# Weight quadrants loaded three steps before their sums, and part of the sums moved from VectorE to GpSimd

## The chip, the cores and the metric

The kernel runs on one core of one Trainium2 chip. The core has TensorE (PE; its weight loads are PEld), VectorE (DVE), ScalarE (ACT), GpSimd (POOL) and SyncE (SP), which work side by side and wait for each other by semaphores; each takes its instructions in order. SP and GpSimd also issue DMAs, which sixteen DMA engines carry out. The metric is the device time of one execution in microseconds. The median of three runs of the kernel before is 2614.47 us (2612.9 to 2618.87).

## The reference

One layer of a decoder trunk over a prompt of 2048 tokens (from position 0, no state) and 64 sample tokens (8 sequences of 8, with state), all in float32:

```
z = rms_norm(x, pre_g);  proj = z @ w_in            # 2048 -> 5 x 1024: xr, gr, u, v, gs
xc = causal depthwise conv of width 4 over xr
r, i = sigmoid(xc @ w_r + b_r), sigmoid(xc @ w_i + b_i)          # 8 heads of 128
h = linear recurrence with a = exp(-8 r softplus(-lam)) over sqrt(1 - a^2) i xc
br = h * silu(gr)
v = rms_norm(gelu(v), sgu_g);  s = (masked w_s) v + b_s          # within chunks of 128 tokens
bs = gelu(u) * s * silu(gs)
y = x + rms_norm([br, bs] @ w_out, post_g)                       # 2048 -> 2048
```

The two large products (`w_in` and `w_out`) hold nearly all of the arithmetic. The outputs are y, the last conv rows and h, and the normalised v of the sample.

## The kernel before

The prompt is worked in four groups of 512 tokens; the first group also takes the 64 sample tokens. A float32 product is made of three passes of TensorE in a rounded format: each weight tile and each activation tile is split into a high half (rounded by ScalarE, line L184 for weights, as `wh_...`) and a low half (the rest, by VectorE, L192, as `wl_...`), and high x high, high x low and low x high are summed.

**Groups 1 to 3** multiply by a scheme with seven products of half-size blocks in place of eight. Of a unit (a 2 x 2 arrangement of weight blocks B11, B12, B21, B22, each 128x1024 here) it needs the four quadrants as they are and the four sums P1 = B11 + B12, P3 = B12 + B22, P2 = B22 + P1 and P4 = B21 + P2. There are 28 units: 16 of column blocks of `w_in` (kind `c`: xr with gr, u with gs), 4 of `w_v` and 8 of `w_or` (the same v and out weights, laid out by rows). The sums are the same for all three groups.

**The first group** multiplies plainly, and makes these sums on the side: `make_sums` loads a unit's four quadrants into SBUF (DMAs issued by GpSimd, line L235), adds them on VectorE (L241, L243, L245, L247), and stores each sum to DRAM (DMAs issued by GpSimd, L239), where later groups load it as they load any weight. The buffers are of the pool `dp` (tag `dbl`, 13 buffers), which the first group also uses for the gelu of v (3 for each of two halves, from the v stage until the spatial products are done), gate weights, squares, and later the statistics of group 1.

The first group's TensorE work goes by steps, one weight piece each (48 matmuls of 128x288, L363; 30 of 128x512 for v, L374). The jobs come in this order: xr and gr by head pairs with gates and recurrence between, v, then gs and u by head pairs with a spatial product for each head (`spatial_pe` L552, taken from PSUM by VectorE in `spatial_dve` L558), then the sixteen blocks of the output projection (`out`). A weight piece is loaded by SP (`wraw_...`, L176), rounded by ScalarE (L184) and has its low half made by VectorE (L192), three pieces ahead (LOOK = 3), in pools of three buffers. VectorE also evacuates products (`scaled`, L393).

Other work on GpSimd's queue in this group is: u times gs (L545), the gate product i times xc (L478), the stores of the branches to DRAM (`cat`, L500 and L578), their reloads ahead of the output projection (`cb`, L336), the stores of its blocks (L590) and the sums of their squares (L311), and from block 8 on the loads for the statistics of group 1 (`xs`, L613). From these statistics VectorE makes `xd` (L630), which TensorE spreads over the partitions (`nsx`, L635).

What sets the order: in the first group the program gives steps and side work in program order, and the framework's scheduler puts every engine's instructions in a fixed order, by priority (program order) and by its own estimate of when each is ready; so an instruction can be put well ahead of its place in the program where its engine and a buffer are free. `by_step` gives the place of each unit: with a clock of 6.3 us for a step (6.8 for v), unit n stands at the first step whose clock is at least 60 + 20.5 n. Groups 1 to 3 are in an order written out by hand (`manual_schedule`), and the change doesn't touch them.

Of the kernel before, what the change touches and what calls it, by code (L numbers as in the profile page):

```python
# [32 lines left out]
W = 1024  # L33
# [18 lines left out]
def hybrid_layer(ctx: ExitStack, tc: tile.TileContext, a):  # L52
    nc = tc.nc
# [18 lines left out]
    def dbl(name, dt=F32):  # L72
        return dp.tile([P, 2, DW], dt, tag="dbl", name=name)

    def flat(t, n):
        return t.rearrange("p a c -> p (a c)")[:, :n]
# [16 lines left out]
    side = nc.gpsimd  # L93
# [47 lines left out]
    state = {}  # L141
# [66 lines left out]
    def cm_src(w, j, i):  # L208
        return a[w][j][:, i * HALF:(i + 1) * HALF, :].rearrange("p a c -> p (a c)")

    def tm_src(w, j, i):
        return a[w][j, i].rearrange("p a c -> p (a c)")
# [6 lines left out]
    def quadrants(unit):  # L219
        kind, j, u = unit  # L220
        if kind == "c":
            return {"B11": cm_src("w_in", j, 0), "B21": cm_src("w_in", j, 1),
                    "B12": cm_src("w_in", j + 1, 0), "B22": cm_src("w_in", j + 1, 1)}
        return {"B11": tm_src(kind, 2 * j, u), "B21": tm_src(kind, 2 * j, 4 + u),
                "B12": tm_src(kind, 2 * j + 1, u), "B22": tm_src(kind, 2 * j + 1, 4 + u)}

    sums = {}

    def make_sums(unit):
        src = quadrants(unit)  # L230
        nm = "_".join(str(x) for x in unit)
        t = {}
        for b in ("B11", "B12", "B22", "B21"):
            t[b] = flat(dbl(f"p{b}{nm}"), W)
            side.dma_start(t[b], src[b])  # L235

        def put(k, x):
            sums[unit, k] = hp.tile([P, W], F32, name=f"{k}_{nm}")
            side.dma_start(sums[unit, k], x)  # L239

        nc.vector.tensor_add(t["B11"], t["B11"], t["B12"])  # L241
        put("P1", t["B11"])
        nc.vector.tensor_add(t["B12"], t["B12"], t["B22"])  # L243
        put("P3", t["B12"])
        nc.vector.tensor_add(t["B22"], t["B22"], t["B11"])  # L245
        put("P2", t["B22"])
        nc.vector.tensor_add(t["B21"], t["B21"], t["B22"])  # L247
        put("P4", t["B21"])

    def prod_src(unit, k):  # L250
# [814 lines left out]
    for s in steps:  # L1065
        for job, i in s:
            kind, j = job
            if is_v(job):
                src = lambda j=j, i=i: tm_src("w_v", j, i)
            else:  # L1070
                src = lambda w="w_out" if kind == "out" else "w_in", j=j, i=i: cm_src(w, j, i)
# [37 lines left out]
    for hp_ in range(0, NH, 2):  # L1109
        i = jobs.index(("gr", NH + hp_ + 1))  # L1110
# [13 lines left out]
    by_step = defaultdict(list)  # L1124
    clock, when = 0.0, []
# [1 line left out]
        when.append(clock)  # L1127
        clock += sum(6.8 if is_v(job) else 6.3 for job, _ in s)
    for n, u in enumerate(units):
        t = 60 + 20.5 * n  # L1130
        by_step[next(i for i, x in enumerate(when) if x >= t)].append((make_sums, u))
    for n in range(8):
        at(("out", 8 + n // 4), stat_load, 1, n)
        at(("out", 9 + n // 4), stat_sum, 1, n)
# [22 lines left out]
    for n, step in enumerate(steps):  # L1157
        for f, *args in by_step[n]:
            f(*args)
        job, i = step[0]  # L1160
# [31 lines left out]
    for g in range(1, NG):  # L1192
# [25 lines left out]
        if g == 1:  # L1218
            for j in range(KT):
                t = 4 + 3 * j // 2 if j < 10 else V + 11 + 2 * (j - 10)  # L1220
                at2(t, finish0_load, j)
                t = max(t + 3, 9)
# [179 lines left out]
```

## Time and profile before

| what | value |
|---|---|
| median of 3 runs | 2614.47 us |
| profiled execution, its own time | 2626.4 us |
| its span, first to last instruction | 2624.7 us |
| granted TensorE clock, mean over the span | 0.981 |
| mean DMA rate over the span | 224 GB/s |
| matmul instructions | 16710 |

The rows further down are of this one profiled execution. Times are microseconds from the start of the span, unless marked ns. The granted clock is a share of full speed: 1.00 is the level of 2.4 GHz, 0.50 that of 1.2 GHz, and a mean between them is a stretch that has both. A wait is the idle time of an engine just before an instruction, and behind the arrow stands what ended it. The first group lasts until about 824 us of the span, when the last block of its output projection is evacuated.

### The profile page before, as it was taken

Reading aid. Unit: us, or ns where it says so; the run is one execution under the profiler, and the core shown is the slowest. Engines: PE = TensorE matmul, PEld = TensorE weight load, DVE = VectorE, ACT = ScalarE, POOL = GpSimd, SP = SyncE. Lnnn points to the kernel's source line nnn. Section 1 sums busy time; section 2 is a strip of 40 time slices with the busy share of each in tenths; the row PEclk is TensorE's granted clock in tenths of the full one; section 3 lists DMA queues with packets and bytes.
Section 4 is the critical chain, followed back from the end, with each engine's and each line's share of the span. In section 5 each row is a group of like instructions: output and inputs, shape, how many; then the busy total and the mean of one; then the engine's idle time right before and its main releaser. Section 6 shows DMA issues by size and latency. Waiting matters only on the chain.

```text
span 2624.7 us, 41603 instructions
## 1 busy us (share of the span) xinstructions
PE 2515.9 (96%) x16710; PEld 2314.8 (88%) x16710; DVE 1761.6 (67%) x2284; ACT 1396.5 (53%) x1787; POOL 350.7 (13%) x504
## 2 busy tenths in 40 slices
PE   7999999899998999999999899999999999999996
PEld 6999789899998998799878898899878898899884
DVE  7786255545457777666789677666789677656865
ACT  5445332123233577645756477645756477645654
POOL 4331023322422200100100200000000200000000
PEclk9999999999998999999999999999999999999998
DMA  6995378865865855756775955555775955555576
GB/s 225 332 336 192 112 256 305 322 255 186 322 241 161 272 179 186 234 184 186 256 263 190 328 171 181 170 184 185 256 257 195 327 178 177 179 182 182 187 260 189
DMA packets 168673, 589.21 MB, mean 224 GB/s; under 512 B 19216, under 2 KB 19776, under 8 KB 168480
## 3 DMA queue, kind: packets, MB, share of 16 engines
q1 hardware_dynamic: 106544, 377.06, 43.1%
q0 software_dynamic: 60784, 207.40, 23.5%
q8 instruction: 130, 2.13, 0.3%
q10 hardware_dynamic: 1152, 2.10, 0.2%
q14 instruction: 63, 0.52, 0.1%
HBM read 494.92 MB, written 89.47 MB: 223 GB/s over the span
## 4 chain that ended last, share of the span: by engine, by line
PE 71%; DMA 10%; DVE 8%; ACT 5%; issue 4%; POOL 1%; SPq 0%; DVEq 0%; ACTq 0%; POOLq 0%
PE gm0out L363 7%; PE gm0v L374 4%; PE gm0gr L363 4%; PE gm0xr L363 2%; PE gm0gs L363 2%; DVE wl_c_B L192 1%; DMA wraw_c_P<-P_c 1%; PE gm0u L363 1%; DMA wraw_w_or_P<-P_w_or 1%; PE g L850 1%; DMA pB22w_v<-w_v 1%; DMA wraw_c_B<-w_in 1%; PE sp L552 1%; PE w3o1a L709 1%; PE w3vd L709 1%
## 5 line engine op out<-in xcount | busy, mean ns | idle before, releaser
L184 ACT ACTIVATE wh_c_P<-wraw_c_P 128x1024 fp32r<-128x1024 f32 x192 | 203.3, 1059 | 269.6 <-DMA wraw_c_P<-P_c 87.4
L192 DVE TENSOR_TENSOR wl_c_P<-wraw_c_P,wh_c_P 128x1024 fp32r<-128x1024 f32 x192 | 234.4, 1222 | 111.8 <-ACT wh_c_P L184 109.0
L192 DVE TENSOR_TENSOR wl_c_B<-wraw_c_B,wh_c_B 128x1024 fp32r<-128x1024 f32 x144 | 175.3, 1220 | 84.1 <-ACT wh_c_B L184 84.1
L184 ACT ACTIVATE wh_c_B<-wraw_c_B 128x1024 fp32r<-128x1024 f32 x144 | 152.1, 1057 | 140.6 <-DMA wraw_c_B<-w_in 46.9
L184 ACT ACTIVATE wh_w_or_P<-wraw_w_or_P 128x1024 fp32r<-128x1024 f32 x96 | 101.6, 1058 | 85.5 <-DMA wraw_w_or_P<-P_w_or 32.3
L192 DVE TENSOR_TENSOR wl_w_or_P<-wraw_w_or_P,wh_w_or_P 128x1024 fp32r<-128x1024 f32 x96 | 117.3, 1222 | 43.8 <-ACT wh_w_or_P L184 43.2
L184 ACT ACTIVATE wh_w_or_B<-wraw_w_or_B 128x1024 fp32r<-128x1024 f32 x72 | 76.3, 1059 | 85.3 <-DMA wraw_w_or_B<-w_or 17.5
L363 PE MATMUL gm0out<-c0l,wh_out 128*128 128x288 f32 x512 | 112.2, 300 | 1.4 <-DVE c0l L158 1.3
L192 DVE TENSOR_TENSOR wl_w_or_B<-wraw_w_or_B,wh_w_or_B 128x1024 fp32r<-128x1024 f32 x72 | 87.9, 1221 | 35.9 <-ACT wh_w_or_B L184 35.5
L363 PE MATMUL gm0out<-c0h,wl_out 128*128 128x288 f32 x512 | 110.8, 298 | 0.1
L363 PE MATMUL gm0out<-c0h,wh_out 128*128 128x288 f32 x512 | 110.7, 298 | 0.0
L363 PEld LDWEIGHTS gm0out<-c0l,wh_out 128*128 128x128 f32 x512 | 82.6, 190 | 2.9 <-DVE c0l L158 2.3
L363 PEld LDWEIGHTS gm0out<-c0h,wl_out 128*128 128x128 f32 x512 | 82.8, 190 | 0.8 <-issue 0.5
L363 PEld LDWEIGHTS gm0out<-c0h,wh_out 128*128 128x128 f32 x512 | 82.7, 190 | 0.1
L613 POOL DMA_DIRECT2D xs<-xt x24 | 12.8, 536 | 504.5 <-ACT wh_c_P L184 257.2
L192 DVE TENSOR_TENSOR wl_w_v_P<-wraw_w_v_P,wh_w_v_P 128x1024 fp32r<-128x1024 f32 x48 | 58.5, 1222 | 27.7 <-ACT wh_w_v_P L184 27.7
L184 ACT ACTIVATE wh_out<-wraw_out 128x1024 fp32r<-128x1024 f32 x32 | 33.7, 1056 | 81.3 <-PE gm0out L363 54.3
L184 ACT ACTIVATE wh_w_v_P<-wraw_w_v_P 128x1024 fp32r<-128x1024 f32 x48 | 49.9, 1054 | 47.2 <-DMA wraw_w_v_P<-P_w_v 31.9
L192 DVE TENSOR_TENSOR wl_out<-wraw_out,wh_out 128x1024 fp32r<-128x1024 f32 x32 | 41.0, 1283 | 41.3 <-ACT wh_out L184 41.2
L363 PE MATMUL gm0xr<-z0h,wh_xr 128*128 128x288 f32 x256 | 57.3, 306 | 7.9 <-ACT wh_xr L184 5.5
L374 PE MATMUL gm0v<-wh_v,z0l 128*128 128x512 f32 (+1 forms) x160 | 63.4, 396 | 0.0
L374 PE MATMUL gm0v<-wl_v,z0h 128*128 128x512 f32 (+1 forms) x160 | 63.1, 394 | 0.0
(1612 smaller groups left out, 8544.5 us busy)
## 6 DMA issues: line engine op xcount, KB each, us to landing
wraw_c_P<-P_c SPq DMA_DIRECT2D x192, 512.0 KB, 4.1
wraw_c_B<-w_in SPq DMA_DIRECT2D x144, 512.0 KB, 4.2
wraw_w_or_P<-P_w_or SPq DMA_DIRECT2D x96, 512.0 KB, 4.3
wraw_w_or_B<-w_or SPq DMA_DIRECT2D x72, 512.0 KB, 4.2
wraw_w_v_P<-P_w_v SPq DMA_DIRECT2D x48, 512.0 KB, 3.6
wraw_w_v_B<-w_v SPq DMA_DIRECT2D x36, 512.0 KB, 3.4
wraw_out<-w_out SPq DMA_DIRECT2D x32, 512.0 KB, 4.6
xs<-xt POOLq DMA_DIRECT2D x24, 512.0 KB, 6.6
```

What stands on the lines that cost most here:

```text
L184: nc.scalar.activation(h[:, sl], raw[:, sl], AF.Copy)
L192: nc.vector.tensor_sub(l[:, sl], raw[:, sl], h[:, sl].bitcast(F32))
L363: nc.tensor.matmul(p[:, :n], w, zz[:, o:o + n], start=(k == 0 and n_pass == 0), stop=(k == KT - 1 and n_pass == 2))
L374: nc.tensor.matmul(p[:n], zz[:, c * P:c * P + n], w, start=(k == 0 and n_pass == 0), stop=(k == KT - 1 and n_pass == 2))
L552: nc.tensor.matmul(p[:, c * P:(c + 1) * P], state["vn", c, h // 4][:, vs], wst[:, h, :], start=True, stop=True)
L613: side.dma_start(x, a[f"xt{g}"][c * P:(c + 1) * P, b * W:(b + 1) * W])
L709: nc.tensor.matmul(bks[b], zz, w, start=(not cont and kk == 0 and n_pass == 0), stop=(kk == HALF - 1 and n_pass == 2), skip_group_check=True)
L850: nc.tensor.matmul(p, ww[:, ws], xx[:, i, :TP], start=n_pass == 0, stop=n_pass == 2)
```

## The change

`make_sums` is parted in two. `load_quadrants` issues the four loads of a unit and stands at the first step whose clock is at least 45 + 20.5 n; `make_sums`, now only the adds and stores, stands at 64 + 20.5 n, three steps further on. The adds of the 16 units of kind `c` stay on VectorE; those of the 4 `w_v` and 8 `w_or` units are made by GpSimd. The number and size of all transfers and adds stay as they are.

```diff
--- before.py
+++ after.py
@@ -226,25 +226,29 @@
 
     sums = {}
 
+    def load_quadrants(unit):
+        src = quadrants(unit)
+        t = state["quad", unit] = {}
+        for b in ("B11", "B12", "B22", "B21"):
+            t[b] = flat(dbl(f"p{b}" + "_".join(str(x) for x in unit)), W)
+            side.dma_start(t[b], src[b])
+
     def make_sums(unit):
-        src = quadrants(unit)
         nm = "_".join(str(x) for x in unit)
-        t = {}
-        for b in ("B11", "B12", "B22", "B21"):
-            t[b] = flat(dbl(f"p{b}{nm}"), W)
-            side.dma_start(t[b], src[b])
+        t = state.pop(("quad", unit))
 
         def put(k, x):
             sums[unit, k] = hp.tile([P, W], F32, name=f"{k}_{nm}")
             side.dma_start(sums[unit, k], x)
 
-        nc.vector.tensor_add(t["B11"], t["B11"], t["B12"])
+        eng = nc.vector if unit[0] == "c" else nc.gpsimd
+        eng.tensor_add(t["B11"], t["B11"], t["B12"])
         put("P1", t["B11"])
-        nc.vector.tensor_add(t["B12"], t["B12"], t["B22"])
+        eng.tensor_add(t["B12"], t["B12"], t["B22"])
         put("P3", t["B12"])
-        nc.vector.tensor_add(t["B22"], t["B22"], t["B11"])
+        eng.tensor_add(t["B22"], t["B22"], t["B11"])
         put("P2", t["B22"])
-        nc.vector.tensor_add(t["B21"], t["B21"], t["B22"])
+        eng.tensor_add(t["B21"], t["B21"], t["B22"])
         put("P4", t["B21"])
 
     def prod_src(unit, k):
@@ -1127,8 +1131,8 @@
         when.append(clock)
         clock += sum(6.8 if is_v(job) else 6.3 for job, _ in s)
     for n, u in enumerate(units):
-        t = 60 + 20.5 * n
-        by_step[next(i for i, x in enumerate(when) if x >= t)].append((make_sums, u))
+        for t, f in ((45 + 20.5 * n, load_quadrants), (64 + 20.5 * n, make_sums)):
+            by_step[next(i for i, x in enumerate(when) if x >= t)].append((f, u))
     for n in range(8):
         at(("out", 8 + n // 4), stat_load, 1, n)
         at(("out", 9 + n // 4), stat_sum, 1, n)
```

## Rows read from the trace of the kernel before

**Rows 1.** The page, busy time of the engines (us, share of the span, instructions).

```profile
PE 2515.9 (96%) x16710; PEld 2314.8 (88%) x16710; DVE 1761.6 (67%) x2284; ACT 1396.5 (53%) x1787; POOL 350.7 (13%) x504
```

**Rows 2.** Windows, line L363 alone: us, PE and PEld busy (instructions), granted clock, DMA.

```profile
168.00:194.00 26.00, 21.84 (x149) 21.13 (x148) 0.93 0.93 325
443.00:552.00 109.00, 89.15 (x629) 87.72 (x629) 0.92 0.89 327
552.00:606.00 54.00, 51.63 (x384) 51.06 (x383) 1.00 0.53 183
627.00:764.00 137.00, 137.00 (x1030) 137.00 (x1029) 1.00 0.79 283
```

**Rows 3.** Waits of TensorE, 436 to 552 us: in total, times, longest.

```profile
PE sp L552 <- DVE s L558: 8.2, 2, 4.2
PE gm0gs L363 <- DVE wl_gs L192: 3.6, 2, 3.1
PE gm0u L363 <- DVE wl_u L192: 2.2, 2, 1.6
```

**Rows 4.** Waits of VectorE, 436 to 552 us.

```profile
DVE pB11w_v L241 <- DMA pB12w_v<-w_v: 17.9, 3, 8.1
DVE pB11w_or L241 <- DMA pB12w_or<-w_or: 13.3, 3, 7.8
DVE pB12w_or L243 <- DMA pB22w_or<-w_or: 7.9, 2, 4.5
DVE pB11w_v L241 <- issue: 7.8, 1, 7.8
DVE pB12w_v L243 <- DMA pB22w_v<-w_v: 4.7, 2, 2.5
```

**Rows 5.** Timeline of VectorE, 448 to 454 us: start, duration, what, [idle before].

```profile
448.98 1.23 DVE L241 TENSOR_TENSOR pB11w_v<-pB11w_v,pB12w_v 128x1024 f32<-128x1024 f32 x1 [8.15 <-DMA pB12w_v<-w_v]
...
451.48 0.81 DVE L393 TENSOR_TENSOR gs<-gm0gs,rsBx 128x288 f32<-128x288 f32 x2
...
452.21 1.21 DVE L192 TENSOR_TENSOR wl_u<-wraw_u,wh_u 128x1024 fp32r<-128x1024 f32 x1
...
453.35 0.74 DVE L558 SCALAR_TENSOR_TENSOR s<-sp,cv,bsb 128x512 f32<-128x512 f32 x1
```

**Rows 6.** DMA issues, 436 to 560 us: times, KB each, median us to landing.

```profile
pB22w_v<-w_v POOLq DMA_DIRECT2D x4, 512.0 KB, 8.9
```

**Rows 7.** Windows, all engines: us, PE, PEld, DVE, ACT, POOL busy, clock, DMA.

```profile
440.00:731.00 291.00, 276.18 (x2001) 272.30 (x2000) 151.85 (x172) 70.28 (x82) 86.99 (x137) 0.97 0.76 276
...
443.00:552.00 109.00, 95.58 (x659) 93.51 (x659) 59.11 (x65) 18.80 (x21) 32.09 (x56) 0.92 0.89 327
```

**Rows 8.** Durations of a line's instructions (ns min/median/max), L241 and L478.

```profile
L241 DVE TENSOR_TENSOR pB11w_or<-pB11w_or,pB12w_or x8: 1224/1225/1227, 515.8 to 725.1; 128x1024 f32<-128x1024 f32 x8
...
L478 POOL TENSOR_TENSOR i<-i,xc x8: 1417/1488/1894, 101.3 to 262.5; 128x576 f32<-128x576 f32 x8
```

**Rows 9.** Timeline of GpSimd.

```profile
487.26 1.61 POOL L545 TENSOR_TENSOR u<-u,gs 128x576 f32<-128x576 f32 x1 [0.18 <-ACT u L544]
...
519.85 0.53 POOL L235 DMA_DIRECT2D pB12w_or<-w_or  x1
...
524.97 0.53 POOL L235 DMA_DIRECT2D pB22w_or<-w_or  x1
...
730.61 0.53 POOL L239 DMA_DIRECT2D P_w_or<-pB21w_or  x1 [0.73 <-DVE pB21w_or L247]
...
733.98 2.10 POOL L613 DMA_DIRECT2D xs<-xt  x4
```

**Rows 10.** Timeline of VectorE, 162 and 487 us.

```profile
162.03 1.23 DVE L241 TENSOR_TENSOR pB11c<-pB11c,pB12c 128x1024 f32<-128x1024 f32 x1 [8.15 <-DMA pB12c<-w_in]
...
487.51 2.44 DVE L247 TENSOR_TENSOR pB21w_v<-pB21w_v,pB22w_v 128x1024 f32<-128x1024 f32 x1
```

**Rows 11.** Waits of TensorE, 750 to 830 us.

```profile
PE nsx L635 <- DVE xd L630: 3.8, 1, 3.8
```

## The prediction

> **What bounds the kernel now.** I read the page first: TensorE is busy 96% of the span, VectorE 67%, GpSimd 13% [rows 1]. So time can be won only where TensorE stands still or is slowed, and only in the first group, since the edit touches nothing behind it. The second view is the windows with the GEMM line L363 alone. In the undisturbed stretch of the out projection 1030 of its matmuls take 137 us, 0.133 us each, and a stretch of the gs/u stage with no sums in it holds 384 in 54 us: 51.1 us by that rate, so its 20 spatial matmuls take the other 2.9 us, 0.147 us each. From 443 to 552 us there are 629 matmuls: 83.7 us, and 30 spatial ones for 4.4 us. The window is 109 us long, so 20.9 us are lost there, part as idle time and part at the lower clock level (the mean grant is 0.92 there and 1.00 in the other two) [rows 2]. In the same way 168 to 194 us loses 26 − 149 × 0.133 = 6.2 us [rows 2].
>
> The third view is who waited in that stretch. TensorE waited for VectorE only: for the take of the spatial product (L558, 8.2 us) and for low halves of weights (L192, 3.6 and 2.2 us) [rows 3]. VectorE in turn waited for quadrants on their way in: 17.9 + 13.3 + 7.9 + 4.7 us for DMAs, and 7.8 us with no releaser shown, before the first add of a w_v unit, which I count as the same: 51.6 us for 7 units, 7.4 us each [rows 4]. The timeline of VectorE shows the chain once: it stands 8.15 us before the add at 448.98; behind it in the queue are the evacuation of gs at 451.48, the low half of a u weight at 452.21 and the spatial take at 453.35 [rows 5]. None of the three needs the quadrants; they are late because the queue is in order. A quadrant takes a median 8.9 us to land there [rows 6], while the transfers take 0.89 of the DMA engines [rows 7].
>
> **The change part by part.**
>
> *Adds of v and out units leave VectorE.* All seven units of the stretch are w_v or w_or units, so every wait of [rows 4] leaves VectorE's queue, and 7 × 4 = 28 adds of 1.225 us [rows 8] with it, 34.3 us. The lost 20.9 us are the upper bound of the gain; the lower bound is none, if something else is late in the same places.
>
> *What is late next: the port.* The same add on GpSimd is not in the trace. The nearest row is its multiply of 128x576: 1417 ns at least, 1894 at most [rows 8]. By columns (1024/576) that is 2.52 to 3.37 us; I take 2.5, the undisturbed end, because the long ones are those that meet VectorE. While GpSimd computed from 487.26 to 488.87, a VectorE add begun at 487.51 took 2.44 us instead of 1.23: it ended 1.08 us after GpSimd did, so VectorE was held until GpSimd was through [rows 9, 10]. The spatial take (one input in PSUM) and the evacuations from PSUM are not two-input reads of SBUF, and I cost them at nothing; the low halves can be held by up to 2.5 us. Of TensorE's waits four are over a microsecond (4.2 and 4.0 for L558, 3.1 and 1.6 for low halves, [rows 3]); at each I leave half an add, 1.25 us, 5 us in all. A low half normally has more room than that: it is made three pieces ahead with three buffers, and one piece is 48 × 0.133 = 6.4 us. So the gain of this part is 20.9 − 5 = 15.9 us.
>
> The GPSIMD Engine Reference of the Trainium skill (section Engine selection) says to put elementwise adds on VectorE, as GpSimd needs about twice the time for two inputs, and its Key points say that the two share their SBUF interfaces when VectorE reads two inputs there. The trace agrees with both (2.5 us by columns against 1.225; 2.44 against 1.23); that the rule speaks against this change is weighed as the second rival.
>
> *The load on GpSimd.* From 440 to 731 us, in which it handles all 12 moved units, GpSimd is busy 87.0 us of 291 [rows 7]. 48 adds × 2.5 us make 120 us more; with each add behind a VectorE instruction in flight (1894 − 1417 = 0.48 us, [rows 8]) 143 us. That is 207 to 230 us of the 270 that are left if 20.9 go: 40 to 63 us spare, 3.3 to 5.3 us for a unit. While GpSimd adds one unit (4 × 2.5 us, and 4 stores of 0.53 us, [rows 9]), some 12 us, the next unit's quadrants land, where the adds on VectorE gave them 4 × 1.225 = 4.9 us. Of a wait of 7.4 us about 0.3 would be left, so I cost it at nothing. If the cover is gone and the 7.4 us stay, 12 × 7.4 = 89 us meet 40 to 63 us of room, and the queue is 26 to 49 us late.
>
> *Loads three steps ahead.* No transfer is added: 28 × 4 loads and as many stores, as before. Program order alone does not set their time: GpSimd takes loads early wherever a buffer is free. In the stretch this is held by buffers: the pool has 13, v of the first group keeps 6, so 7 are left for units of 4. The trace shows it: the second quadrant of the next unit is issued at 519.85, the third only at 524.97, behind stores of the unit before [rows 9]. With the edit the limit is the same: three of four quadrants can run ahead. Each load still waits in GpSimd's queue for its buffer, and the multiply of u with gs, the stores of branches and the reloads for the out projection stand behind it, as now. I take nothing for it.
>
> *The 16 units of column blocks.* Their adds stay on VectorE. There, at 162.03, one of them waits 8.15 us for a quadrant [rows 10], and behind that lie the 6.2 us lost from 168 to 194. By the new order that wait may go (−6.2) or another like it may come (+6.2): ten units in the first 210 us run as far ahead as buffers allow in both kernels. I take 0, the middle.
>
> *The end of the group.* Loads of the statistics of group 1 begin at 733.98, right behind the last store of the last unit at 730.61 [rows 9], and TensorE later waits 3.8 us for what is made of them (nsx, [rows 11]). With the stretch 15.9 us shorter the out projection begins and ends earlier, and the units must end as much earlier; by the spare time above they do.
>
> Sum, on the profiled execution: 2626.4 us (span 2624.7 and 1.7 around it) − 15.9 = 2610.5. That execution lies 11.9 us above the median of the runs, 2614.47; against that the forecast is 2614.5 − 15.9 = 2598.6.
>
> **The rivals.**
>
> 1. *Both stretches are cleared.* The hold costs nothing and the wait at 162 goes: −20.9 − 6.2 = −27.1, 2587.4 us. For it: the trace has TensorE waiting for VectorE only. Against it: column-block adds still wait for quadrants on VectorE.
>
> 2. *The port gives back what the wait cost.* 28 adds × 2.5 = 70 us in which VectorE can be held, in place of 34.3 + 51.6 = 85.9 us of work and wait. If TensorE's loss follows VectorE's, 20.9 × 70/85.9 = 17.0 stay: −3.9, 2610.6 us. For it: the hold in [rows 9, 10] lasted to the end of GpSimd's instruction. Against it: the take for which TensorE waited longest reads PSUM, and a hold is 2.5 us where the wait was 8. Against it too: VectorE is busy only 59 of the 109 us [rows 7]. By the Trainium skill's rule on engine selection (above) this is the likelier case; the trace bears it out for single instructions, and for no stage.
>
> 3. *GpSimd's queue becomes the bound; slower.* One mechanism: each unit still waits for its quadrants, now in GpSimd's in-order queue, with the loads of the statistics behind the last unit. It decides once the wait for a unit is above 3.3 to 5.3 us; then the excess goes one for one into TensorE's wait for nsx. At 7.4 us, the backlog is 26 to 49, middle 37.5 us: −20.9 + 37.5 = +16.6, 2631.1 us. For it: the quadrants' landing time and the buffers stay as they are. Against it: 12 us of adds cover the next landing.
>
> **How the numbers follow.** The forecast has a chance of 0.50, the rivals 0.10, 0.22 and 0.18. The forecast's own range is 2591 to 2607. The range for 8 in 10 reaches over most of the first rival, 2588, and into the third, whose own span is 2619.6 to 2642.6, to 2628; about 0.11 of it is left out above, and 0.05 of the first below. About 0.2% (5.2 us) is what a measurement of this kernel can tell from no change. Faster by more: 0.47 of the forecast, 0.10, 0.06 of the second rival: 0.63. Within: 0.03, 0.12 of the second, 0.03 of the third: 0.18. Slower: 0.04 and 0.15: 0.19.
>
> **What would show it.** Right: from 443 us over the same 629 matmuls the window shrinks from 109 to some 93 us, VectorE has no wait for quadrants of w_v or w_or, and the granted clock there is near 1.00. GpSimd's adds take 2.5 to 3.4 us, and the low halves that meet them some 2.4 us or more. The units end before the evacuation of the ninth out block. Wrong: low halves or the take L558 still end TensorE's waits with VectorE held (second rival); GpSimd waits over 5 us for each unit, and nsx ends a wait far above 3.8 us (third); or new waits for quadrants before 210 us move the sum by 6 us each way.

## The result, and the profile after

| | before | after |
|---|---|---|
| median of 5 runs each, taken side by side (us) | 2618.87 (2612.9 to 2620.77) | 2599.67 (2598.45 to 2604.44) |
| ratio, with 95% interval | | 0.9932 [0.9918, 0.9946] |
| span of the profiled execution (us) | 2624.7 | 2596.8 |
| granted TensorE clock over the span | 0.981 | 0.988 |

The change makes the kernel faster by (1 − 0.9932) × 2618.87 = 17.8 us, 14.1 to 21.5 by the interval. The line of the page that answers to [rows 1]:

```profile
PE 2502.2 (96%) x16710; PEld 2303.2 (89%) x16710; DVE 1737.8 (67%) x2236; ACT 1398.3 (54%) x1787; POOL 468.0 (18%) x552
```

48 adds went from VectorE to GpSimd (2284 to 2236 and 504 to 552 instructions). Where the time went is seen best by the starts of TensorE's steps. The table is read from the timeline of TensorE: first matmul of one step to first matmul of another, in us ("gs 7" is the eighth gs step; v, out and the others likewise).

| stretch of the first group | before | after | what lies there |
|---|---|---|---|
| start to gr 3 | 77.50 | 75.16 | prologue |
| gr 3 to v 0 | 178.65 | 181.30 | xr and gr, column-block sums on VectorE |
| v 0 to gs 7 | 187.20 | 186.40 | v, first gs and u |
| gs 7 to gs 12 | 108.57 | 87.56 | v and out sums |
| gs 12 to out 21 | 194.04 | 193.23 | last gs and u, out |
| out 21 to out 31 | 71.62 | 71.44 | statistics of group 1 come in |
| behind out 31 | 1807.13 | 1801.65 | groups 1 to 3, same code |

One stretch carries it, 21.0 us. The windows of L367 alone (L363 of before), as [rows 2]: us, PE and PEld busy with counts, granted clock, DMA share, GB/s.

```profile
168.00:194.00 26.00, 23.32 (x176) 23.08 (x175) 1.00 0.89 307
443.00:552.00 109.00, 104.27 (x776) 103.32 (x775) 1.00 0.97 353
```

In the same 109 us stand 776 GEMM matmuls in place of 629, at a clock of 1.00 in place of 0.92. Of the 20.9 us that the prediction counts as lost there, 13.4 were idle time of TensorE (busy 95.58 of 109 us in [rows 7]); the other 7.5 lay in matmuls that ran while the granted clock was lower. With all engines, as [rows 7]: PE, PEld, DVE, ACT and POOL busy.

```profile
440.00:731.00 291.00, 289.98 (x2165) 287.95 (x2164) 131.74 (x122) 78.25 (x92) 201.58 (x187) 1.00 0.78 278
443.00:552.00 109.00, 109.00 (x816) 108.25 (x815) 59.83 (x44) 27.99 (x29) 103.88 (x90) 1.00 0.97 353
```

TensorE is busy for all of it. It has no wait left there (the waits of [rows 3] are all gone), GpSimd went from 32 to 104 us of 109, and the DMA share from 0.89 to 0.97. VectorE's waits from 436 to 552 us, as [rows 4]: total, times, longest.

```profile
DVE wl_gs L192 <- ACT wh_gs L184: 16.8, 8, 5.2
DVE wl_u L192 <- ACT wh_u L184: 10.9, 9, 3.3
DVE gs L397 <- PE gm0gs L367: 10.6, 4, 4.2
DVE u L397 <- PE gm0u L367: 10.1, 3, 3.5
```

No quadrant is among them. VectorE now waits for ScalarE's high halves and for TensorE itself: it is ahead of its work. GpSimd's timeline shows how the quadrants come (start, duration, what):

```profile
476.36 2.41 POOL L245 TENSOR_TENSOR pB11w_v<-pB11w_v,pB12w_v 128x1024 f32<-128x1024 f32 x1
478.72 0.57 POOL L234 DMA_DIRECT2D pB11w_or<-w_or  x1
479.29 0.53 POOL L242 DMA_DIRECT2D P_w_v<-pB11w_v  x1
479.84 2.40 POOL L247 TENSOR_TENSOR pB12w_v<-pB12w_v,pB22w_v 128x1024 f32<-128x1024 f32 x1
482.17 0.58 POOL L234 DMA_DIRECT2D pB12w_or<-w_or  x1
...
711.59 0.57 POOL L242 DMA_DIRECT2D P_w_or<-pB21w_or  x1 [0.30 <-POOL pB21w_or L251]
...
714.09 2.12 POOL L617 DMA_DIRECT2D xs<-xt  x4
```

The loads of the next unit (`pB11w_or`, 478.72) go between the adds of this one, so its first add, at 491.69, needs no wait. In the out stage it is otherwise. GpSimd's waits from 560 to 800 us (total, times, longest):

```profile
POOL pB11w_or L245 <- DMA pB12w_or<-w_or: 18.3, 4, 5.3
```

Each of the four units there still waits for its quadrants. The last store of the last unit is at 711.59 and the statistics' loads begin at 714.09; in [rows 9] these were 730.61 and 733.98. Counted from the start of out 0 (585.87 us, before 607.50) the last store is 125.7 us in where it was 123.1: beside TensorE's work the units end later than before. The wait of [rows 11] is as it was:

```profile
PE nsx L639 <- DVE xd L634: 3.8, 1, 3.8
```

The 5.5 us behind out 31 are not counted to the change: in the ten experiments below, whose groups 1 to 3 are the same code, that part takes 1799.6 to 1805.1 us. The profiled execution of before is a long one, and the ratio of the runs is the measure. Of e9's five runs, one with a granted clock of 0.75 took 3041.26 us and is not in its ratio.

### The profile page after: what moved, and what is told of

The parts are those of the page before. It is cut to its first block, busy times and chain, and to the rows that moved or that the text cites. A ratio compares the mean times of both kernels' runs of the same rounds, so it can differ in the third digit from the quotient of the medians.

```text
span 2596.8 us, 41550 instructions
## 1 busy us (share of the span) xinstructions
PE 2502.2 (96%) x16710; PEld 2303.2 (89%) x16710; DVE 1737.8 (67%) x2236; ACT 1398.3 (54%) x1787; POOL 468.0 (18%) x552
## 4 chain that ended last, share of the span: by engine, by line
PE 70%; DMA 9%; DVE 8%; ACT 5%; issue 5%; POOL 3%; SPq 0%; DVEq 0%; ACTq 0%; POOLq 0%
PE gm0v L378 4%; PE gm0gs L367 4%; PE gm0u L367 4%; PE gm0out L367 3%; PE gm0gr L367 3%; PE gm0xr L367 2%; DVE wl_c_B L192 1%; PE g L854 1%; PE sp L556 1%; DMA pB12c<-w_in 1%; DMA wraw_c_P<-P_c 1%; PE w3vd L713 1%; PE w2o1a L713 1%; PE w1o1d L713 1%; PE w3o1a L713 1%
## 5 line engine op out<-in xcount | busy, mean ns | idle before, releaser
L192 DVE TENSOR_TENSOR wl_c_B<-wraw_c_B,wh_c_B 128x1024 fp32r<-128x1024 f32 x144 | 175.4, 1221 | 85.4 <-ACT wh_c_B L184 85.4
L184 ACT ACTIVATE wh_w_or_B<-wraw_w_or_B 128x1024 fp32r<-128x1024 f32 x72 | 76.2, 1059 | 80.4 <-DMA wraw_w_or_B<-w_or 24.5
L367 PE MATMUL gm0out<-c0l,wh_out 128*128 128x288 f32 x512 | 111.7, 299 | 1.0 <-DVE c0l L158 0.8
L367 PE MATMUL gm0out<-c0h,wl_out 128*128 128x288 f32 x512 | 110.5, 297 | 0.5 <-DVE wl_out L192 0.4
L367 PE MATMUL gm0out<-c0h,wh_out 128*128 128x288 f32 x512 | 110.4, 297 | 0.0
L617 POOL DMA_DIRECT2D xs<-xt x24 | 12.8, 536 | 504.7 <-ACT wh_c_P L184 257.3
L192 DVE TENSOR_TENSOR wl_out<-wraw_out,wh_out 128x1024 fp32r<-128x1024 f32 x32 | 48.2, 1507 | 64.4 <-ACT wh_out L184 64.4
L367 PEld LDWEIGHTS gm0out<-c0l,wh_out 128*128 128x128 f32 x512 | 82.4, 189 | 2.3 <-DVE c0l L158 1.7
L367 PEld LDWEIGHTS gm0out<-c0h,wl_out 128*128 128x128 f32 x512 | 82.4, 189 | 1.5 <-DVE wl_out L192 1.0
L367 PEld LDWEIGHTS gm0out<-c0h,wh_out 128*128 128x128 f32 x512 | 82.2, 189 | 0.1
L367 PE MATMUL gm0gr<-z0h,wl_gr 128*128 128x288 f32 x256 | 56.9, 304 | 7.1 <-DVE wl_gr L192 7.1
L367 PE MATMUL gm0xr<-z0h,wh_xr 128*128 128x288 f32 x256 | 56.6, 302 | 7.2 <-ACT wh_xr L184 5.1
```

The lines of the kernel that those rows point to most:

```text
L184: nc.scalar.activation(h[:, sl], raw[:, sl], AF.Copy)
L192: nc.vector.tensor_sub(l[:, sl], raw[:, sl], h[:, sl].bitcast(F32))
L367: nc.tensor.matmul(p[:, :n], w, zz[:, o:o + n], start=(k == 0 and n_pass == 0), stop=(k == KT - 1 and n_pass == 2))
L617: side.dma_start(x, a[f"xt{g}"][c * P:(c + 1) * P, b * W:(b + 1) * W])
```

## The experiments

The change has two parts, and the table sets each against the kernel before, with the stretches that differ (us, from the same step starts; "xs" is when GpSimd issues the first load of the statistics, counted from the start of out 0).

| kernel | ratio to before, 95% | gr 3 to v 0 | gs 7 to gs 12 | xs | out 21 to 31 |
|---|---|---|---|---|---|
| before | 1 | 178.65 | 108.57 | 126.5 | 71.62 |
| after | 0.9932 [0.9918, 0.9946] | 181.30 | 87.56 | 128.2 | 71.44 |
| e1, adds moved only | 0.9997 [0.9985, 1.0009] | 175.37 | 87.54 | 151.1 | 90.83 |
| e2, early loads only | 0.9993 [0.9982, 1.0005] | 181.20 | 105.95 | 122.2 | 66.39 |
| e3, column adds on GpSimd too | 1.0007 [0.9996, 1.0019] | 198.25 | 87.56 | 129.4 | 72.14 |
| e4, GpSimd's work doubled | 1.0272 [1.0255, 1.0288] | 180.41 | 87.56 | 175.8 | 98.87 |
| e5, e1 with one unit early | 0.9959 [0.9947, 0.9972] | 177.94 | 87.54 | 138.3 | 77.58 |
| e6, after with one unit late | 0.9935 [0.9916, 0.9954] | 180.13 | 87.56 | 124.5 | 69.79 |
| e7, e1, statistics' loads on SP | 0.9940 [0.9922, 0.9958] | 178.42 | 87.54 | on SP | 73.20 |
| e8, after, statistics' loads on SP | 0.9921 [0.9898, 0.9944] | 183.69 | 87.56 | on SP | 66.41 |
| e9, e8 with column loads late | 0.9902 [0.9888, 0.9917] | 179.91 | 87.54 | on SP | 66.40 |
| e10, after with column loads late | 0.9921 [0.9906, 0.9935] | 178.59 | 87.54 | 128.3 | 72.53 |

The theories of the first four: A, the place of the adds in VectorE's in-order queue was the cost; B, the early loads are the gain; C, a VectorE held by GpSimd is not free.

### One part at a time

e1 moves the adds and leaves loads and adds of a unit together:

```diff
-        for t, f in ((45 + 20.5 * n, load_quadrants), (64 + 20.5 * n, make_sums)):
-            by_step[next(i for i, x in enumerate(when) if x >= t)].append((f, u))
+        t = 60 + 20.5 * n
+        by_step[next(i for i, x in enumerate(when) if x >= t)].append((make_sums, u))
```

> Only the engine is changed: w_v and w_or units are added on GpSimd, and loads and adds stand together at 60 + 20.5 n as before the change. Theory A (the adds' place in VectorE's in-order queue was the cost): the stretch of the gs/u stage loses under 2 us of the 20.9, no wait of VectorE for w_v or w_or quadrants is left, and the time is that of the changed kernel within 5 us: 2595 to 2605 us. Theory B (the earlier loads were the gain): the quadrants still land late, GpSimd stands some 7 us for each unit, and at least half of the 20.9 us stays: 2608 us or more. The loss of the first 210 us can differ by some 6 us either way in both.

e2 keeps the early loads and leaves all adds on VectorE:

```diff
-        eng = nc.vector if unit[0] == "c" else nc.gpsimd
+        eng = nc.vector
```

> Only the loads are moved: quadrants are loaded at 45 + 20.5 n and added at 64 + 20.5 n, all on VectorE. Theory A: buffers hold the loads back as before, VectorE still waits some 40 to 52 us for quadrants of the seven units of the stretch, and TensorE still loses 15 us or more there: 2609 to 2622 us. Theory B: the quadrants have landed when VectorE comes to them, those waits fall under 15 us, and the time is that of the changed kernel: 2595 to 2605 us.

Measured: 2617.41 and 2615.35 us against 2617.91 of before. Neither part alone gains anything that can be told from none, and both together gain 17.8 us. A missed on e1: the stretch is cleared, as it says, but the time didn't come. B missed on e2, and on e1 its time came (2608 us or more) without its reason. VectorE's waits of e2 from 436 to 552 us show why the early loads are not enough there:

```profile
DVE pB11w_v L245 <- DMA pB12w_v<-w_v: 17.9, 3, 7.7
DVE pB11w_or L245 <- DMA pB12w_or<-w_or: 11.0, 3, 7.1
DVE pB12w_or L247 <- DMA pB22w_or<-w_or: 8.5, 3, 4.2
```

These are nearly those of [rows 4]: with the adds on VectorE, loads placed three steps ahead still don't land in time. In e1 the stretch is cleared as in the changed kernel (87.54 us), and the loss has gone to the out stage. TensorE's and ScalarE's waits of e1, 690 to 800 us:

```profile
PE gm0out L364 <- ACT wh_out L184: 17.0, 1, 17.0
...
ACT xs L622 <- DMA xs<-xt: 36.9, 5, 31.7
```

GpSimd's waits of e1, 560 to 800 us:

```profile
POOL pB11w_or L242 <- DMA pB12w_or<-w_or: 30.3, 5, 6.9
```

and the timelines of GpSimd and ScalarE there:

```profile
719.71 2.39 POOL L242 TENSOR_TENSOR pB11w_or<-pB11w_or,pB12w_or 128x1024 f32<-128x1024 f32 x1 [5.40 <-DMA pB12w_or<-w_or]
...
733.94 2.10 POOL L614 DMA_DIRECT2D xs<-xt  x4
...
740.64 1.06 ACT L622 ACTIVATE xs<-xs 128x1024 f32<-128x1024 f32 x1 [31.68 <-DMA xs<-xt]
...
743.16 1.04 ACT L184 ACTIVATE wh_out<-wraw_out 128x1024 fp32r<-128x1024 f32 x1
```

GpSimd has five units in the out stage (first adds at 623.1, 647.2, 672.0, 694.7 and 719.7 us), each with its own wait of 5.4 to 6.9 us for quadrants; in the stretch of the v and out sums its units need none behind the first, just as in the changed kernel. The statistics' loads stand behind the fifth; ScalarE stands 31.7 us before their squares, and behind these in its queue is the high half of an out weight, for which TensorE waits 17.0 us. The changed kernel has four units there.

### More work on GpSimd

e3 gives GpSimd the adds of the column blocks too (`eng = nc.gpsimd`).

> The changed kernel with the adds of the 16 column-block units on GpSimd too. Theory A, carried on to the first 210 us: TensorE's 9 us that the changed kernel still loses there, in two places behind VectorE's waits for quadrants, go with those waits, as far as GpSimd keeps up; 40 adds of 2.4 us, 96 us, come to a queue that is busy about a third of those 160 us: 2588 to 2598 us. Theory C (holding VectorE is not free where VectorE is busy four fifths of the time, as it is there): VectorE is held up to 96 us in place of 49 us of adds, the low halves come late again, and the loss of that stretch stays or grows: 2599 to 2615 us.

e4 follows each moved add by two products of 768 and 256 columns that nothing reads:

```diff
+                nc.gpsimd.tensor_mul(idle, x[:, :768], x[:, :768])
+                nc.gpsimd.tensor_mul(idle[:, :256], x[:, 768:], x[:, 768:])
```

> The changed kernel in which each of the 48 moved adds is followed on GpSimd by two products of the same tile (768 and 256 columns) that nobody reads; outputs stay as they are. GpSimd is busy 104 of 109 us in the stretch of the changed kernel, so this asks for what a slower queue costs. If the queue has the room that the prediction gave it (40 to 63 us), 48 more instructions of about 2.5 us, 120 us, put it 57 to 80 us late at the statistics' loads, and TensorE's wait for nsx grows from 3.8 us by about that: 2650 to 2680 us. If the stages take the lateness up elsewhere (units that end later harm nothing until groups 1 to 3 read the sums), the time stays within 10 us of the changed kernel: 2595 to 2610 us.

Measured: 2618.88 and 2687.21 us. e3 came out above the expectations of both A and C, and e4 7 us above the dearer of its two. From gr 3 to v 0 e3 takes 198.25 − 181.30 = 17.0 us more than the changed kernel. TensorE's waits for VectorE there, e3 first:

```profile
PE gm0gr L367 <- DVE wl_gr L192: 15.1, 7, 5.8
...
PE gm0gr L367 <- DVE wl_gr L192: 7.1, 2, 4.4
```

VectorE has no wait for quadrants left, and though 64 adds are gone from it, it is busy 170.3 of 198 us there, where it was 132.5 of 181. Groups of VectorE there, 165 to 215 us (busy, mean ns, idle before):

```profile
L421 DVE SCALAR_TENSOR_TENSOR xc<-xsm,cv,xc 128x64 f32<-128x64 f32 x6 | 9.3, 1557 | 0.0
L158 DVE TENSOR_TENSOR xcl<-xc,xch 128x576 fp32r<-128x576 f32 x2 | 6.6, 3318 | 0.0
```

An operation of 64 columns takes 1557 ns on average; in the changed kernel the same group is

```profile
L421 DVE SCALAR_TENSOR_TENSOR xc<-xsm,cv,xc 128x64 f32<-128x64 f32 x6 | 1.7, 279 | 0.0
```

So holding VectorE costs time where it has many short operations in a row, as C says. In gs 7 to gs 12 it costs nothing: 87.56 us even in e4, with low halves there at a mean of 3041 and 2325 ns. e4's cost is elsewhere, by TensorE's waits from 560 to 840 us:

```profile
PE gm0out L378 <- ACT c0h L157: 38.9, 1, 38.9
PE gm0out L378 <- ACT wh_out L184: 24.6, 2, 24.5
PE sp L567 <- DVE s L573: 13.5, 1, 13.5
PE gm0u L378 <- DVE wl_u L192: 5.2, 2, 4.1
```

38.9 us are for the first activations of the out projection, whose reloads `cb` are issued by GpSimd from 628.9 us on, among the adds of its eighth unit (in the changed kernel from 562.6), and 24.5 us are e1's wait again. The 13.5 us come at the next spatial product, behind those activations. The 5.2 us are VectorE's in-order queue once more, now with a wait for GpSimd's product of u and gs (L560) in it and a low half behind that:

```profile
568.59 1.16 DVE L590 TENSOR_TENSOR u<-u,s 128x576 f32<-128x576 f32 x1 [21.36 <-POOL u L560]
569.66 1.21 DVE L192 TENSOR_TENSOR wl_u<-wraw_u,wh_u 128x1024 fp32r<-128x1024 f32 x1
```

I had expected a late nsx; GpSimd's queue was late in three places ahead of it.

### What the early loads do

Theory D: they matter only because one more unit then runs in front of the out stage, so the statistics' loads are in time. Rival E: every unit needs its quadrants ahead. e5 puts that one unit early in e1, e6 puts it back in the changed kernel; e7 takes the statistics' loads out of GpSimd's queue in e1, and e8 in the changed kernel.

e5, against e1:

```diff
-        t = 60 + 20.5 * n
+        t = (45 if n == 23 else 60) + 20.5 * n
```

e6, against the changed kernel:

```diff
-        for t, f in ((45 + 20.5 * n, load_quadrants), (64 + 20.5 * n, make_sums)):
+        for t, f in (((60 if n == 23 else 45) + 20.5 * n, load_quadrants), (64 + 20.5 * n, make_sums)):
```

e7, against e1, and e8, against the changed kernel:

```diff
-        side.dma_start(x, a[f"xt{g}"][c * P:(c + 1) * P, b * W:(b + 1) * W])
+        (nc.sync if g == 1 else side).dma_start(x, a[f"xt{g}"][c * P:(c + 1) * P, b * W:(b + 1) * W])
```

> Loads and adds of a unit stand together again as in the kernel before, v and out adds are on GpSimd, and one unit alone, the one that falls to time 516.5 or 531.5, is put 15 earlier, so that it comes before the first out block. Theory D (loads three steps ahead matter only because they bring this one unit in front of the out stage; then GpSimd is through before the statistics' loads are due): the same time as the changed kernel, 2595 to 2603 us, GpSimd handles four units behind the first out block and not five, and TensorE has no wait of some 17 us for ScalarE in the out stage. Rival E (each unit needs its quadrants ahead, also behind the first out block): 2609 to 2618 us, as with the engine moved alone, and the wait in the out stage stays above 8 us.

> The changed kernel, with the loads of that same unit put back to time 531.5, so that it comes behind the first out block; all other loads stay three steps ahead. Theory D: five units are left for GpSimd behind the first out block, the statistics' loads come late, and most of the gain is lost: 2609 to 2620 us, with a wait of TensorE of 8 us or more about the third row of out blocks. Rival E: the other eleven units' early loads carry the gain: 2597 to 2604 us.

> The engine moved alone (loads and adds together), with one edit more: the loads of the statistics of group 1 are issued by SP and not by GpSimd, so they don't stand behind the last unit in GpSimd's queue. If the lateness of those loads in GpSimd's queue is what took the gain of the move, 15 to 20 us come back: 2594 to 2604 us, and TensorE's wait for ScalarE in the out stage of 17 us is gone. If something else takes it (the units' own sums late for the next group's weights, or the hold of VectorE by GpSimd): 2610 to 2620 us.

> The changed kernel with the loads of the statistics of group 1 issued by SP. If GpSimd still makes them late there, some 4 to 8 us more come back: 2591 to 2597 us, with the wait for nsx of 3.8 us gone. If they come in time already: the same as the changed kernel, 2597 to 2602 us.

Measured: 2606.96, 2600.64, 2601.78 and 2594.91 us against 2615.83 of before. e7 decides the first question: with nothing else altered, taking those loads off GpSimd turns e1's ratio of 0.9997 into 0.9940, and the wait of 17.0 us is gone. So the statistics' loads behind late units are what took the gain of the move. D and E each hold for a part. e5 gains 0.0038 of e1's missing 0.0065, between the ranges of D and E; e6 keeps the whole gain with five units in the out stage, against D. GpSimd's timeline of e6 shows the other way:

```profile
624.85 2.38 POOL L245 TENSOR_TENSOR pB11w_or<-pB11w_or,pB12w_or 128x1024 f32<-128x1024 f32 x1 [4.35 <-DMA pB12w_or<-w_or]
627.19 0.57 POOL L234 DMA_DIRECT2D pB11w_or<-w_or  x1
...
640.73 2.40 POOL L245 TENSOR_TENSOR pB11w_or<-pB11w_or,pB12w_or 128x1024 f32<-128x1024 f32 x1
...
710.49 2.15 POOL L617 DMA_DIRECT2D xs<-xt  x4
```

The next unit's load goes behind the first add of this one, its adds start without a wait, and units follow each other in 15.9 to 19.9 us, where e1 needs 22.7 to 25.0 (e1 has no unit loaded ahead there: its loads at 638.20 to 639.78 are followed by a wait of 6.88 us at 647.18). One unit fewer, or shorter units: either way the loads come in time. Lateness beyond that costs: from the changed kernel to e5 the xs loads come 10.1 us later and out 21 to out 31 grows by 6.1 us, and from there on it is paid one for one. From e5 to e1 the loads come 151.1 − 138.3 = 12.8 us later, and the stretch grows by 90.83 − 77.58 = 13.3 us; from e1 to e4 they come 7.9 us later, counted from the start of out 21, and it grows by 8.0. Why the changed kernel's own four units in the out stage don't run ahead as e6's do was not traced.

e8 takes the stretch from out 21 to 31 from 71.44 to 66.41 us, and the wait for nsx from 3.8 to 1.3. That is 5 us in one profile; the interval of its runs overlaps that of the changed kernel, so by the runs alone the gain over it is not shown. As much is lost in before: it takes 71.62 us there, and e2, with these loads at 122.2, takes 66.39.

### The column blocks' loads, and the best version

e9 (with SP's loads) and e10 (without) put the column units' loads back beside their adds:

```diff
+        lo, su = (60, 60) if u[0] == "c" else (45, 64)
+        for t, f in ((lo + 20.5 * n, load_quadrants), (su + 20.5 * n, make_sums)):
```

> The changed kernel with two edits: the loads of the 16 column-block units stand together with their adds again at 60 + 20.5 n, as in the kernel before (the twelve v and out units keep the early loads and GpSimd's adds), and SP issues the loads of the statistics of group 1. If the early column-block loads are what costs the 6.2 us at the ninth xr step (139 to 144 us) in the changed kernel, that loss goes, with the 3 us that they win at the second gr step behind it coming back: a net 2 to 4 us below the kernel with SP's loads alone, 2588 to 2596 us. If that loss is only where the wait for a quadrant happens to fall: 2593 to 2600 us.

> The changed kernel with only the loads of the 16 column-block units put back beside their adds. If the early column-block loads cost by themselves, 2594 to 2599 us and no step of 13 us at the ninth xr; if they win as much as they cost, 2598 to 2602 us, as the changed kernel.

Measured: 2593.26 and 2599.33 us against 2618.59 of before. e9's time lies in both of its ranges and decides nothing; by runs e10 is the changed kernel again, so its gain doesn't hang on the early loads of column blocks. Over the profiles there is a difference: from gr 3 to v 0 the five kernels with early column loads and the adds on VectorE (after, e2, e4, e6, e8) take 180.1 to 183.7 us, mean 181.3, and the six with late ones (before, e1, e5, e7, e9, e10) 175.4 to 179.9, mean 178.1; up to gr 3 the early ones are ahead by 77.0 − 75.8 = 1.2 us in the mean. One loss is in all five and in none of the six: the step ahead of the ninth xr takes 12.9 to 13.5 us, where it is 7.19. As other steps win by the early loads, the net is some 2 us by these means, an estimate that the runs don't show: e1, e5 and e7, whose code is the same up to the out stage, spread over 3 us from gr 3 to v 0. e9 is the fastest by its median, and faster than before: 0.9902 [0.9888, 0.9917]. Its interval lies just below that of the changed kernel, which was taken beside other runs of before, and overlaps those of e8 and e10.

## Why the prediction was right

Forecast 2598.6 us, measured 2599.67; forecast gain 15.9, measured 17.8 us. That the times differ by 1.1 us alone is partly luck: the level of before was 4.4 us higher than the 2614.47 that the forecast started from, and the gain was larger too. And one of its reasons is missing from the sum: as that took nothing for the early loads, it gives e1 the same 2598.6 us, and e1 measured 2617.41. Step by step:

- **Adds leave VectorE.** Right, and the upper bound came: all 20.9 us predicted as lost in the stretch are back (21.0 by step starts), and e1 shows that this part alone clears it.
- **The 5 us left for the hold** were mis-sized: nothing was left. The hold itself is there, and larger than a single add. Groups of VectorE after, 443 to 552 us:

```profile
L192 DVE TENSOR_TENSOR wl_gs<-wraw_gs,wh_gs 128x1024 fp32r<-128x1024 f32 x8 | 24.4, 3053 | 16.8 <-ACT wh_gs L184 16.8
L192 DVE TENSOR_TENSOR wl_u<-wraw_u,wh_u 128x1024 fp32r<-128x1024 f32 x8 | 17.4, 2175 | 10.7 <-ACT wh_u L184 10.7
...
L562 DVE SCALAR_TENSOR_TENSOR s<-sp,cv,bsb 128x512 f32<-128x512 f32 x4 | 3.0, 740 | 0.0
```

  Low halves take 3053 and 2175 ns in place of 1214 and 1216. The spatial take, with an input in PSUM, stays at 740, as reckoned. The prediction left half an add at each wait that had been seen; but those waits came from the queue, and once it was empty the low halves were begun so early that 1 to 2 us more in the mean reached nobody.
- **An add on GpSimd** was put at 2.5 us, and measured 2.4; durations of L245 (ns min/median/max):

```profile
L245 POOL TENSOR_TENSOR pB11w_or<-pB11w_or,pB12w_or x8: 2384/2399/2412, 491.7 to 697.0; 128x1024 f32<-128x1024 f32 x8
L245 POOL TENSOR_TENSOR pB11w_v<-pB11w_v,pB12w_v x4: 2397/2408/2430, 430.8 to 476.4; 128x1024 f32<-128x1024 f32 x4
```

- **The load on GpSimd** at nothing: right in cost for this kernel, but its reason holds in one stage only. GpSimd was busy 201.6 us from 440 to 731 (two whole adds lie ahead of that, from 430.8 on), against 207 to 230 reckoned. That the adds of one unit cover the next unit's loads came true in the stretch, where units behind the first wait for nothing. In the out stage the four units wait 4.6 us each in the mean, where 0.3 were reckoned and trouble was to begin at 3.3 to 5.3. And the sign that the units end before the evacuation of the ninth out block failed: their stores end at 712.16, this evacuation at 705.35 (before, 731.14 and 731.04). GpSimd did fall behind; with four units left the stage could take it.
- **"Loads three steps ahead: I take nothing for it"** is the step that failed, and the sum hid it. Without the early loads the kernel stands at 0.9997 (e1): with the statistics' loads on GpSimd, the whole 17 us hang on them. They keep the third rival away, as e7 shows, which gains 0.0060 without them. The argument that buffers limit how far loads run fits e2; it did not ask what they do for GpSimd's last units.
- **Third rival.** Its mechanism is real: in e1's out stage units wait 5 to 7 us each for quadrants, in GpSimd's queue, the statistics' loads come late, and beyond e5 the excess is paid one for one. It was placed at nsx; it came earlier, through ScalarE's queue (`wh_out` behind `xs`). It was priced at 16.6 us over before; e1 shows none, since the 17.1 + 2.7 us that it loses ahead of out 22 and 23 and the stretch's 21 cancel.
- **Second rival.** By the Trainium skill (GPSIMD Engine Reference, Engine selection) an elementwise add belongs on VectorE. The prices agree (2.40 us against 1.225), but the time went against this rule in the stretch of the v and out sums, where VectorE is busy 60 of 109 us, and with it in e3, where the column adds on GpSimd cost 17 us.
- **Column blocks** at 0 ± 6.2: one loss of 6.2 us came just ahead of the ninth xr step (13.35 us where 7.19 were) and 3.5 went at two gr steps after it, within the bounds.
- **A reading.** The 8.9 us to landing are those of the third of a unit's four loads; the medians of the four in that stretch are 5.7, 7.7, 8.9 and 9.5 us. The sum doesn't use them.

## What to carry to other kernels

An operation that waits for a DMA holds all that stands behind it in its engine's queue, so a slower engine with free time can be the better place for it; but then read what stands behind it in the new queue. Moving work and loading for it early were worth nothing alone and 17.8 us together: price the last item of the new queue, and what is issued behind it, before calling a load's place free. Here short operations in a row, on an engine busy four fifths of the time, suffered from the hold; long ones with slack didn't.

## What the runs showed of the hardware

VectorE is held not by one GpSimd instruction only. Timelines of the changed kernel, GpSimd first:

```profile
470.91 1.44 POOL L549 TENSOR_TENSOR u<-u,gs 128x576 f32<-128x576 f32 x1
472.29 0.60 POOL L242 DMA_DIRECT2D P_w_v<-pB22w_v  x1
472.91 2.40 POOL L251 TENSOR_TENSOR pB21w_v<-pB21w_v,pB22w_v 128x1024 f32<-128x1024 f32 x1
...
471.00 5.41 DVE L192 TENSOR_TENSOR wl_gs<-wraw_gs,wh_gs 128x1024 fp32r<-128x1024 f32 x1 [2.99 <-ACT wh_gs L184]
```

The low half begun at 471.00 lasts over both GpSimd operations and the 0.6 us between them, and ends at 476.41, 1.10 us after the second: 5.41 us for 1.22. In the changed kernel GpSimd pays next to nothing for it: all 48 adds take 2380 to 2480 ns. But an add that begins inside a running operation of VectorE can be held in its turn. In e1, VectorE first:

```profile
625.79 1.23 DVE L192 TENSOR_TENSOR wl_out<-wraw_out,wh_out 128x1024 fp32r<-128x1024 f32 x1 [0.19 <-ACT wh_out L184]
...
626.37 2.90 POOL L244 TENSOR_TENSOR pB12w_or<-pB12w_or,pB22w_or 128x1024 f32<-128x1024 f32 x1
```

The add took 2.90 us for 2.40 and ended 2.25 us after the low half, which kept its 1.23; the longest add of e4 took 3.44 us. Nor are operations with two inputs the only ones held: in e3 a copy of 3 columns of `xr` (L405), begun at 171.67 us while GpSimd added from 171.44 to 174.03, took 2.38 us.
